# Two chained transformer blocks on one core: longer give-way times between the steps of the woven attention items

## Chip, cores and metric

The kernel runs as one program on one core of a Trainium2 chip. The metric is the device time of one execution in microseconds (us), where lower is better. The kernel before takes 3177.6 us, the median of three runs.

## What is computed

The reference runs two blocks in sequence on 512 tokens of width 1024, all in float32. The change touches only the attention part of the first block:

```
h = h + 0.5 * swiglu(rmsnorm(h))                       # feed-forward 1
u = rmsnorm(h)
(nq, kc, vc, ksl, vsl, kwn, vwn, ng, sq, sk, sv, ga, gb) = split(u @ w_in)
o_a = nsa(nq, ...)      # 8 heads, 2 key groups: compressed + selected + window attention, gated
o_b = banded(sq, sk, sv, window=128, sinks)            # 8 heads, 1 key head
merged = sigmoid(ga) * (o_a @ w_branch_a) + sigmoid(gb) * (o_b @ w_branch_b)
h = h + merged @ w_out
h = h + 0.5 * swiglu(rmsnorm(h))                       # feed-forward 2
...                                                    # then the second block
```

With 512 tokens, 8 selection blocks and 16 picks, the selected branch sees every earlier token, and so does the window branch with its window of 512. Both are plain causal attention here. The second block (a gated recurrence, a state-space model and a layer of 16384 small experts) follows and is not touched.

## The kernel before

Activations are kept transposed, 128 features by 512 tokens to a tile. Each weight tile of 128x1024 is loaded, split into a rounded part `whi` (ScalarE, line 171) and a rest `wlo` (VectorE, line 172), and multiplied in three passes by `mm3`: a product of a full weight tile, called a projection below, is 24 matmuls of 512 columns on TensorE.

The attention stage is written as Python generators that the planner `weave` interleaves while the program is built. There is one main stream and a list of 20 items. Main does the projections in a fixed order. Those before the items are the compression inputs, the keys, the queries and the four `natural`-layout tiles. Then come two compression products (`compress`, 48 matmuls of 256 columns each), five projections for the banded branch (`sk`, `s0` to `s3`), sixteen projections for the branch gates (lines 800 to 804), eight half-length products of the banded branch's output (`ob`), eight of the other branch (`oa`, lines 805 to 817), and the output projection. Each projection of main hands back after every six matmuls.

An item is the attention of one 128-token query tile for one branch: `full_item` (12 of them), `cmp_item` (compressed keys, 4) and `swa_item` (banded, 4). The order of query tiles is 3, 2, then the four banded items, then 1 and 0. At most two items are open at a time. An item emits all of its scores and its softmax (max and scaling on VectorE, exp on ScalarE), then yields. Then it goes into `attend`: it transposes the probabilities of the first block of 128 keys on TensorE (line 86) and copies them out of PSUM (`evac`, line 654, ScalarE and VectorE in turn), then yields. After that, for each block of keys it emits the next block's transposes and copies and this block's value product on TensorE, and yields.

A yield carries a number of nanoseconds on the planner's own clock `clk`. That clock does not run with time: it goes forward only when something is emitted on TensorE, by the cost that `mm` and `tr` put on it.

```
p = 4 if lhsT.dtype == F32 else 1
self.clk += max(n * 0.4217 * p, m * 0.84 * (2 if p == 4 else 1))    # mm: n columns, m columns of lhsT
...
self.clk += 54                                                      # tr
...
due[0] = v if callable(v) else self.clk + (v or 0)                  # weave, after an item yields v
```

So a yield of 5500 says: do not come back before 5500 ns' worth of other TensorE work was emitted, which is the other open item's or main's. `weave` always takes an item that is due before it takes main; if nothing but items is left it moves the clock on. By this clock one full projection costs 24 x 512 x 0.4217 ns = 5.18 us. The order of emission is the order of priority on each engine's queue.

Working tiles of 128x512 come from one set of 44 buffers (tag `t2k`), PSUM from 8 banks (tag `ps`). The gate projections leave one `t2k` tile each that lives until its branch product.

Of the kernel before, what the change touches and what calls it, by code (L numbers as in the profile page):

```python
# [49 lines left out]
class Prog:  # L50
# [165 lines left out]
    def small(self, n, w=4):  # L216
        t = self.big.tile([128, 64], F32, tag="rs_small", bufs=3, name=self.name("rs"))
        return [t[:, w * i:w * i + w] for i in range(n)]
# [439 lines left out]
    def attend(self, box, col, probs, width, v_of):  # L658
        if "po" not in box:
            box["po"] = self.ps()  # L660
        po = box["po"]
        nb = max(1, width // 128)
        nh = len(probs[0])
        n = min(128, width)
        cs = slice(col, col + 128 * nh)

        def turn(kb):
            r = []
            pts = [self.ps(), self.ps()]
            for pt, pr in zip(pts, probs):  # L670
                for i, p in enumerate(pr):
                    self.transposed(pt, i, p[:, kb * 128:kb * 128 + n], n)
            for pt in pts:
                s = self.t2k()
                self.evac(s[:n, :128 * nh], pt[:n, :128 * nh])
                r.append(s)
            return r

        t = turn(0)
        yield 1200  # L680
        for kb in range(nb):
            nxt = turn(kb + 1) if kb + 1 < nb else None
            start = not box["begun"]
            box["begun"] = True
            box["left"] -= 1
            for i in range(2):
                self.mm(po[64 * i:64 * i + 64, cs], lhsT=v_of(i, kb), rhs=t[i][:n, :128 * nh], start=start,
                        stop=box["left"] == 0)
            t = nxt
            if box["left"] == 0:  # L690
                box["done"]()
            yield 900

    def attention(self, st, done):
        nc, A, ph = self.nc, self.A, self.ph
# [151 lines left out]
        def cmp_item(box, qt):  # L847
            qs = slice(qt * 128, (qt + 1) * 128)
            m8 = small([128, 8, 31], "cm", 2)
            scs = [self.ps(), self.ps()]  # L850
            s4 = [sc[:, 0:128].rearrange("p (r n) -> p r n", r=4)[:, :, 0:31] for sc in scs]
            for r in range(4):
                for g, gp in enumerate(gps):
                    self.mm(s4[g][:, r, :], lhsT=nq[r][gp, qs], rhs=kcc[gp, g, :], start=True, stop=True)
            for g in range(2):
                nc.vector.tensor_tensor(m8[:, 4 * g:4 * g + 4], s4[g],
                                        self.misc["cmp"][:, qt, :][:, None, :].to_broadcast([128, 4, 31]), op=ALU.add)
            mx = small([128, 8], "mx", 6)
            sums = small([128, 8], "sums", 6)
            nc.vector.tensor_reduce(mx, m8, axis=AX.X, op=ALU.max)  # L860
            nc.vector.tensor_scalar(mx, mx, -0.125, None, op0=ALU.mult)
            for r in range(8):
                nc.scalar.activation(m8[:, r, :], m8[:, r, :], AF.Exp, bias=mx[:, r:r + 1], scale=0.125,
                                     accum_out=sums[:, r:r + 1])
            f = small([128, 8], "fac", 6)
            nc.vector.reciprocal(f, sums)
            nc.vector.tensor_tensor(f, f, gates[:, qt, 0:8], op=ALU.mult)
            if qt == 0:
                nc.vector.tensor_tensor(f, f, self.misc["vis"].to_broadcast([128, 8]), op=ALU.mult)
            nc.vector.tensor_tensor(m8, m8, f[:, :, None].to_broadcast([128, 8, 31]), op=ALU.mult)  # L870
            yield 4500
            yield from self.attend(box, 0, [[m8[:, 4 * g + r, :] for r in range(4)] for g in range(2)], 31,
                                   lambda g, kb: vcc[:, g, :])

        def full_item(box, qt, br, heads):
            qs = slice(qt * 128, (qt + 1) * 128)
            kT, off = ((ksl, 0), (kwn, 128))[br]
            nk = (qt + 1) * 128
            nh = len(heads)
            per = max(1, 512 // nk) if nk != 384 else 1  # L880
            mx = small([128, 8], "mx", 6)
            sums = small([128, 8], "sums", 6)
            probs = [[], []]
            for i in range(0, nh, per):
                scs = [self.ps(), self.ps()]
                for j in range(per):
                    for sc, gp in zip(scs, gps):
                        self.mm(sc[:, j * nk:(j + 1) * nk], lhsT=nq[heads[i + j]][gp, qs], rhs=kT[gp, :nk],
                                start=True, stop=True)
                for g, sc in enumerate(scs):  # L890
                    s3 = sc[:, :per * nk].rearrange("p (h n) -> p h n", h=per)
                    nc.vector.tensor_tensor(s3[:, :, qs], s3[:, :, qs],
                                            mdiag[:, None, :].to_broadcast([128, per, 128]), op=ALU.add)
                    k = g * nh + i
                    ms = mx[:, k:k + per]
                    nc.vector.tensor_reduce(ms, s3, axis=AX.X, op=ALU.max)  # L896
                    nc.vector.tensor_scalar(ms, ms, -0.125, None, op0=ALU.mult)
                    p = self.t2k()
                    for j in range(per):
                        pj = p[:, j * nk:(j + 1) * nk]  # L900
                        nc.scalar.activation(pj, s3[:, j, :], AF.Exp, bias=mx[:, k + j:k + j + 1], scale=0.125,
                                             accum_out=sums[:, k + j:k + j + 1])
                        probs[g].append(pj)
            f = small([128, 8], "fac", 6)
            nc.vector.reciprocal(f[:, :2 * nh], sums[:, :2 * nh])
            c = 8 * br + 8
            fv = f[:, :2 * nh].rearrange("p (g r) -> p g r", g=2)
            gv = gates[:, qt, c:c + 8].rearrange("p (g r) -> p g r", g=2)[:, :, heads[0]:heads[0] + nh]
            nc.vector.tensor_tensor(fv, fv, gv, op=ALU.mult)
            for g in range(2):  # L910
                for r in range(nh):
                    nc.vector.tensor_scalar(probs[g][r], probs[g][r], f[:, g * nh + r:g * nh + r + 1], None, op0=ALU.mult)
            yield 5500
            yield from self.attend(box, 128 * heads[0], probs, nk,
                                   lambda g, kb: nat[:, kb, off + g * 64:off + g * 64 + 64])

        def swa_item(box, qt):
# [34 lines left out]
            for par in range(2):  # L952
                for r in range(4):
                    nc.vector.tensor_scalar(probs[par][r], probs[par][r], f[:, 4 * par + r:4 * par + r + 1], None,
                                            op0=ALU.mult)
            yield 6000
            yield from self.attend(box, 0, probs, nw, lambda par, kb: nat[:, ks.start // 128 + kb, 256:320])

        items = []
# [3 lines left out]
        for qt in self.att_order:  # L963
            if qt >= 4:
                items.append((swa_item(accum(ob, "ob", qt - 4, 1 if qt == 4 else 2), qt - 4), need_s))
                continue
            hs = [range(4)] if qt < 2 else [range(0, 2), range(2, 4)]
            box = accum(oa, "oa", qt, 2 * (qt + 1) * len(hs) + 1)
            for br in range(2):
                for h in hs:  # L970
                    items.append((full_item(box, qt, br, list(h)), need))
            items.append((cmp_item(box, qt), need_c))
# [938 lines left out]
```

## Time and profile before

| | |
|---|---|
| median of three runs | 3177.6 us (3174.46 to 3178.54) |
| the profiled execution | 3182.49 us, of which the span of its instructions is 3180.5 us |
| TensorE (PE) | busy 3061.3 us, 96% of the span |
| VectorE (DVE) | busy 2044.6 us, 64% |
| ScalarE (ACT) | busy 1164.7 us, 37% |
| GpSimd (POOL) | busy 1084.8 us, 34% |
| mean granted TensorE clock | 0.98 of full |

The share of busy time is an average over stages. The attention stage runs from about 395 to 835 us of the span. A stop of TensorE is idle time ahead of one of its instructions; the profile names what ended it. The granted clock has two levels, 1.2 and 2.4 GHz, and a window's figure is the mean over its time.

### The profile page before, as it was taken

The page shows a single profiled execution, that of the slowest core. Times are in us where ns is not written, and L with a number is a line of the kernel's source. Part 1 is how long each engine was busy: PE and PEld are TensorE (multiplying, and loading weights), DVE is VectorE, ACT ScalarE, POOL GpSimd, SP SyncE. Part 2 cuts the span into 40 slices and gives each one's busy share as a digit, 9 for nine tenths or more (in the row PEclk, how much of TensorE's full clock was granted, in tenths as well). Part 3 has the DMA queues.
Part 4 walks back from the last instruction along what each step waited for, and adds up shares of the span by engine and source line. Part 5 has one row for each costly group of instructions (what it writes and reads, how often), then busy time and mean ns, then how long its engine had stood idle before and what let it go on. Part 6 is the DMA issues. An engine that isn't in the chain of part 4 may idle for free.

```text
span 3180.5 us, 39943 instructions
## 1 busy us (share of the span) xinstructions
PE 3061.3 (96%) x14672; PEld 2493.6 (78%) x14672; DVE 2044.6 (64%) x3733; ACT 1164.7 (37%) x1851; POOL 1084.8 (34%) x993
## 2 busy tenths in 40 slices
PE   8999998889999999999999988999999999999998
PEld 7888875567777778878888777888887788888887
DVE  7445466754657565864665899888883666555653
ACT  4222334442422224543433343445453333322332
POOL 1000110001222222431254689878771533223321
PEclk9999999999999999989999999999999999999999
DMA  6344331112435444221333344555556765555642
GB/s 197 118 131 136 94 96 47 34 47 86 160 101 170 131 141 133 85 77 54 100 121 116 103 150 168 189 188 188 191 186 225 244 200 184 185 194 193 201 135 78
DMA packets 145059, 443.53 MB, mean 139 GB/s; under 512 B 20177, under 2 KB 22257, under 8 KB 139745
## 3 DMA queue, kind: packets, MB, share of 16 engines
q1 hardware_dynamic: 82512, 285.41, 28.0%
q10 hardware_dynamic: 51968, 111.57, 9.7%
q0 software_dynamic: 10384, 44.01, 4.5%
q8 instruction: 116, 1.90, 0.2%
q14 instruction: 79, 0.64, 0.1%
HBM read 361.88 MB, written 77.86 MB: 138 GB/s over the span
## 4 chain that ended last, share of the span: by engine, by line
PE 78%; DVE 11%; issue 4%; ACT 2%; POOL 2%; DMA 2%; ACTq 0%; SPq 0%; DVEq 0%; POOLq 0%
PE ps L82 77%; DVE wlo L172 2%; DVE b L1543 1%; PE ps L86 1%; DMA aw<-ada_w 1%; ACT whi L171 1%; DVE stage L1568 1%; DMA act_d<-t 1%; DVE sel L1526 0%; DVE mx L896 0%; POOL t L814 0%; DVE aa L521 0%; ACTq L1156 0%; POOL a L1542 0%; DVE eq L1519 0%
## 5 line engine op out<-in xcount | busy, mean ns | idle before, releaser
L171 ACT CAST whi<-raw 128x1024 fp32r<-128x1024 f32 (+2 forms) x505 | 516.6, 1025 | 1210.2 <-PE ps L82 918.3
L82 PE MATMUL ps<-xhi,whi 128*128 128x512 f32 (+1 forms) x2232 | 879.0, 395 | 26.0 <-ACT whi L171 14.5
L82 PE MATMUL ps<-xhi,wlo 128*128 128x512 f32 (+1 forms) x2232 | 868.1, 390 | 8.2 <-DVE wlo L172 8.2
L82 PE MATMUL ps<-xlo,whi 128*128 128x512 f32 (+1 forms) x2232 | 869.4, 390 | 0.8 <-DVE xlo L380 0.7
L172 DVE TENSOR_TENSOR wlo<-raw,whi 128x1024 fp32r<-128x1024 f32 (+2 forms) x470 | 596.7, 1270 | 161.2 <-ACT whi L171 151.4
L82 PEld LDWEIGHTS ps<-xhi,whi 128*128 128x128 f32 x2232 | 425.4, 191 | 117.2 <-ACT whi L171 15.4
L82 PEld LDWEIGHTS ps<-xhi,wlo 128*128 128x128 f32 x2232 | 424.3, 190 | 99.3 <-DVE wlo L172 10.5
L82 PEld LDWEIGHTS ps<-xlo,whi 128*128 128x128 f32 x2232 | 425.2, 191 | 81.4 <-issue 2.1
L1542 POOL TENSOR_SCALAR a<-iota,routeT 128x128 fp32r<-128x128 f32 x512 | 439.6, 874 | 103.1 <-PE ps L82 97.2
L82 PE MATMUL ps<-pwl,whi 128*128 128x512 f32 (+1 forms) x1048 | 408.6, 390 | 2.8 <-DVE pwl L589 2.8
L82 PE MATMUL ps<-pwh,whi 128*128 128x512 f32 (+1 forms) x1048 | 406.8, 388 | 3.3 <-ACT pwh L588 3.2
L82 PE MATMUL ps<-pwh,wlo 128*128 128x512 f32 (+1 forms) x1048 | 403.1, 385 | 0.0
L1660 POOL TENSOR_TENSOR t<-t,gt 128x512 f32<-128x512 f32 x128 | 201.5, 1593 | 419.2 <-DMA t<-act_d 317.7
L1543 DVE SCALAR_TENSOR_TENSOR b<-iota,routeT,routeG 128x256 fp32r<-128x256 f32 x512 | 251.8, 541 | 46.0 <-PE ps L82 46.0
L82 PEld LDWEIGHTS ps<-pwh,whi 128*128 128x128 f32 x1048 | 197.4, 188 | 48.1 <-ACT pwh L588 4.6
L1794 DVE SCALAR_TENSOR_TENSOR h<-ps,mod,h 128x512 f32<-128x512 f32 (+1 forms) x131 | 96.3, 735 | 214.8 <-PE ps L82 214.8
L82 PEld LDWEIGHTS ps<-pwl,whi 128*128 128x128 f32 x1048 | 197.6, 189 | 42.3 <-DVE pwl L589 4.5
L82 PEld LDWEIGHTS ps<-pwh,wlo 128*128 128x128 f32 x1048 | 197.4, 188 | 42.5 <-DVE wlo L172 0.4
L1567 ACT COPY stage<-ps 128x256 f32<-128x256 f32 x256 | 138.1, 643 | 174.3 <-PE ps L82 138.1
L589 DVE TENSOR_TENSOR pwl<-t,pwh 128x512 fp32r<-128x512 f32 x128 | 144.8, 1160 | 40.0 <-ACT pwh L588 35.9
L266 POOL TENSOR_TENSOR acc<-acc,sq 128x512 f32<-128x512 f32 x18 | 32.3, 1796 | 391.2 <-ACT sq L262 390.8
L1568 DVE TENSOR_TENSOR stage<-stage,ps 128x256 f32<-128x256 f32 x256 | 147.3, 623 | 8.2 <-ACT stage L1567 8.1
(401 smaller groups left out, 3859.6 us busy)
## 6 DMA issues: line engine op xcount, KB each, us to landing
raw<-pu SPq DMA_DIRECT2D x128, 512.0 KB, 3.5
raw<-pv SPq DMA_DIRECT2D x128, 512.0 KB, 3.5
act_d<-t ACTq DMA_DIRECT2D x128, 256.0 KB, 2.4
gates_d<-stage ACTq DMA_DIRECT2D x32, 1024.0 KB, 4.6
gt<-gates_d POOLq DMA_DIRECT2D x16, 2048.0 KB, 14.6
t<-act_d ACTq DMA_DIRECT2D x128, 256.0 KB, 3.6
aw<-ada_w SPq DMA_DIRECT2D x48, 512.0 KB, 4.5
raw<-g SPq DMA_DIRECT2D x44, 512.0 KB, 3.6
```

The costliest lines, as they stand in the source:

```text
L82: self.nc.tensor.matmul(out, lhsT=lhsT, rhs=rhs, start=start, stop=stop)
L86: self.nc.tensor.transpose(out, x, ident)
L171: nc.scalar.copy(hi[:, :n], raw[:, :n])
L172: (nc.gpsimd if self.pool_lo else nc.vector).tensor_tensor(lo[:, :n], raw[:, :n], hi[:, :n].bitcast(F32), op=ALU.subtract)
L266: nc.gpsimd.tensor_tensor(st["acc"], st["acc"], sq, op=ALU.add)
L589: self.nc.vector.tensor_tensor(lo, x, hi.bitcast(F32), op=ALU.subtract)
L1542: g.tensor_scalar(a[:, i, :], iota, T2[0][:, c], None, op0=ALU.is_equal)
L1543: v.scalar_tensor_tensor(b[:, i], iota[:, None, :].to_broadcast([128, 2, 128]), T2[1][:, c], TG[:, t + i, :, None].to_broadcast([128, 2, 1 ...
L1567: nc.scalar.copy(sv, pv[:, :, 0])
L1568: v.tensor_tensor(sv, sv, pv[:, :, 1], op=ALU.add)
L1660: g.tensor_tensor(f(t), f(t), gts[e // 8][:, :, e % 8, :], op=ALU.mult)
L1794: nc.vector.scalar_tensor_tensor(x, ps, P.mod[:, 40 + d:41 + d], x, op0=ALU.mult, op1=ALU.add)
```

## The change

Five numbers that the items yield are raised: between softmax and transposes for each of the three kinds of item, between the first transposes and what follows them, and between blocks of keys. Nothing else is edited; the instructions are the same, and their order on the engines is what differs.

```
@@ attend
         t = turn(0)
-        yield 1200
+        yield 2200
         for kb in range(nb):
...
-            yield 900
+            yield 1800
@@ cmp_item
-            yield 4500
+            yield 7000
             yield from self.attend(box, 0, ...)
@@ full_item
-            yield 5500
+            yield 7000
             yield from self.attend(box, 128 * heads[0], probs, nk, ...)
@@ swa_item
-            yield 6000
+            yield 7500
             yield from self.attend(box, 0, probs, nw, ...)
```

## Rows read from the trace of the kernel before

**Rows 1.** Page, part 1: busy us, share of the span, instructions.
```profile
PE 3061.3 (96%) x14672; PEld 2493.6 (78%) x14672; DVE 2044.6 (64%) x3733; ACT 1164.7 (37%) x1851; POOL 1084.8 (34%) x993
```

**Rows 2.** Windows: stretch, its length, busy us by engine, granted clock, DMA.
```profile
454.80:688.00 233.20, 203.01 (x1070) 127.62 (x1069) 164.61 (x468) 112.79 (x356) 6.38 (x5) 0.93 0.15 45
688.00:768.00 80.00, 80.00 (x349) 65.60 (x350) 31.66 (x44) 23.69 (x36) 0.00 (x0) 1.00 0.25 79
410.00:454.80 44.80, 44.46 (x216) 37.22 (x216) 21.76 (x26) 10.52 (x17) 9.39 (x6) 1.00 0.26 83
```

**Rows 3.** TensorE groups by shape, 454.8 to 688 us.
```profile
L82 PE MATMUL ps<-xhi,whi 128*128 128x512 f32 x89 | 40.0, 450 | 1.8 <-ACT t L901 1.8
...
L82 PE MATMUL ps<-xhi,wlo 128*128 128x512 f32 x89 | 38.1, 428 | 0.0
L82 PE MATMUL ps<-xlo,whi 128*128 128x512 f32 x89 | 37.8, 425 | 0.0
...
L82 PE MATMUL ps<-whi,t 128*62 128x256 f32 x61 | 13.0, 293 | 0.0
L82 PE MATMUL ps<-wlo,t 128*62 128x256 f32 x30 | 8.6, 285 | 0.6 <-DVE wlo L172 0.6
```

**Rows 4.** TensorE groups by shape, 688 to 768 us.
```profile
L82 PE MATMUL ps<-xhi,wlo 128*128 128x512 f32 x80 | 31.2, 391 | 0.0
L82 PE MATMUL ps<-xlo,whi 128*128 128x512 f32 x79 | 30.7, 389 | 0.0
L82 PE MATMUL ps<-xhi,whi 128*128 128x512 f32 x79 | 30.7, 389 | 0.0
```

**Rows 5.** Waits of TensorE, 454.8 to 688 us: in total, times, longest.
```profile
PE ps L82 <- ACT t L654: 10.9, 6, 3.9
PE ps L86 <- DVE cm L870: 3.5, 1, 3.5
PE ps L86 <- DVE t L912: 2.7, 3, 1.5
PE ps L86 <- DVE t L954: 2.7, 1, 2.7
PE ps L86 <- ACT t L588: 2.6, 1, 2.6
PE ps L82 <- ACT t L901: 2.3, 3, 1.8
PE ps L82 <- ACT t L944: 2.1, 2, 1.4
PE ps L86 <- ACT t L901: 2.1, 2, 1.9
```

**Rows 6.** Timeline of VectorE and TensorE around the longest stop.
```profile
526.39 0.55 DVE L896 TENSOR_REDUCE mx<-ps 128x1 f32<-128x384 f32 x1
...
527.12 1.21 DVE L172 TENSOR_TENSOR wlo<-raw,whi 128x1024 fp32r<-128x1024 f32 x1
...
528.90 0.41 DVE L654 COPY t<-ps 128x256 f32<-128x256 f32 x1
...
530.00 1.12 PE L82 MATMUL ps<-t,nat 128*64 128x256 f32 x4 [3.90 <-ACT t L654]
```

**Rows 7.** Windows of 5 us around two stops.
```profile
525.00:530.00 5.00, 1.10 (x8) 0.62 (x6) 4.55 (x14) 3.27 (x9) 0.00 (x0) 0.90 0.16 17
530.00:535.00 5.00, 5.00 (x16) 2.81 (x17) 2.11 (x7) 0.60 (x2) 0.00 (x0) 0.50 0.24 91
535.00:540.00 5.00, 5.00 (x26) 2.96 (x25) 1.45 (x3) 0.75 (x2) 1.26 (x1) 0.92 0.00 0
...
655.00:660.00 5.00, 1.97 (x20) 0.97 (x16) 3.89 (x13) 3.28 (x21) 0.00 (x0) 1.00 0.00 0
660.00:665.00 5.00, 4.58 (x23) 3.08 (x24) 3.64 (x14) 3.52 (x17) 0.00 (x0) 1.00 0.00 0
```

**Rows 8.** VectorE and ScalarE groups by shape, 454.8 to 688 us.
```profile
L172 DVE TENSOR_TENSOR wlo<-raw,whi 128x1024 fp32r<-128x1024 f32 x20 | 25.4, 1272 | 2.1 <-ACT whi L171 1.9
...
L802 DVE TENSOR_TENSOR t<-ps,rb 128x512 f32<-128x512 f32 x5 | 3.3, 665 | 0.0
...
L171 ACT CAST whi<-raw 128x1024 fp32r<-128x1024 f32 x20 | 20.9, 1051 | 8.6 <-PE ps L82 7.8 <-ACT t L944 0.5 <-ACT whi L171 0.3
...
L803 ACT ACTIVATE t<-t 128x512 f32<-128x512 f32 x5 | 3.2, 636 | 2.8 <-DVE mx L861 2.0 <-DVE fac L909 0.5 <-DVE t L802 0.4
```

## The prediction, written before the change was run

> **What bounds the kernel now.** I read the page's busy shares first. The reader is to see that TensorE is busy for 96% of the span [rows 1], so that only time in which it stops, or runs at the lower clock, is to be had. Then I cut the attention stage into windows [rows 2]. Before the items (410 to 454.8 us) TensorE is busy 44.46 of 44.80 us, and after them (688 to 768 us) 80.00 of 80.00 us, both at clock 1.00. Between, while the 20 items are open, it is busy 203.0 of 233.2 us at a mean clock of 0.93. All loss that the change can touch lies there: 30.2 us idle, and, since 7% of the clock is missing, 0.07 x 233.2 = 16.3 us of work that would not be there at full clock. Together 46.5 us, 1.5% of the kernel. This is the most that can be gained.
>
> Third, the groups of TensorE instructions say who filled that window: 3 x 89 = 267 matmuls of main's projections, or 11.1 projections, and 61 + 30 = 91 of compression [rows 3]. In the window behind it 79 + 80 + 79 = 238 projection matmuls remain, 9.9 gate projections, with no stop at all [rows 4]. So main has work in hand when the items end, at a place where it covers nothing.
>
> Fourth, the waits name the stops [rows 5]: value products wait 10.9 us for the copies of line 654; transposes wait 3.5 + 2.7 + 2.7 + 2.6 + 2.1 = 13.6 us for probabilities in eight stops; scores and others wait 2.3 + 2.1 = 4.4 us for exps that release what they need. These are the three places at which an item yields too little, except the last, which has no yield.
>
> **What the change adds in cover.** On the planner's clock the yields of all items add up before to: halves of tile 3, 4 x (5.5 + 1.2 + 4 x 0.9) = 41.2; of tile 2, 4 x 9.4 = 37.6; tile 1, 2 x 8.5 = 17.0; tile 0, 2 x 7.6 = 15.2; compressed, 4 x 6.6 = 26.4; banded, 8.1 + 3 x 9.0 = 35.1; in all 172.5 us. The change adds 12 x 1.5 + 4 x 2.5 + 4 x 1.5 between softmax and transposes, 20 x 1.0 behind the first transposes and 45 x 0.9 behind blocks: 34 + 20 + 40.5 = 94.5 us.
>
> The items' own cost on that clock does not change. A half of tile 3, for one, has 4 scores of 512 columns at 0.864 us, 16 transposes at 0.054 and 8 value products of 256 at 0.432: 7.77 us. All items come to 31.1 + 23.3 + 15.5 + 7.8 + 27.2 + 15.5 = 120.4 us. Two items are open at a time, so the stretch grows by half of 94.5, 47.2 us, and as the items' work is fixed, main fills all of it: 47.2 / 5.18 = 9.1 projections.
>
> Does this clock describe the trace? Main's part of the window is 267 x 0.216 + 91 x 0.108 + 5 rotations at 0.864 = 71.7 us, with the items 192.1 us. Two slots of that are 384.2 us, of which 172.5 are yields and 120.4 own work. The remaining 91.3 us are 85 returns that came late, 1.1 us each, which is what main's grain of six matmuls (1.3 us) and the other item's bursts make. I keep them; 20 us more or less would be 10 us, two projections.
>
> Main's work is therefore moved, not added: 9.1 x 24 = 219 matmuls, at 80.00 us / 349 = 0.229 us each [rows 2] 50.1 us, leave the window behind and enter the items' window. The sum there is zero but for the stops and the clock. Of the 9.9 projections 0.8 remain behind the items, and then 96 matmuls of the `ob` product, 22 us, in front of the `oa` product that needs the last item. That tile's copies and splits are some eight operations of this size on either engine, 0.64 to 0.67 us each by the nearest rows [rows 8], so they stay hidden; with main used up they would cost about 5 us.
>
> **What the cover is worth, stop by stop.** If a moved matmul costs the waiting step nothing, each stop shrinks by its own yield's increase. The six stops on line 654 give at most 1.0 each, 6.0. The stop of 3.5 on the compressed item gives 2.5, the three of 2.7 in all (none over 1.5) all of it, the stops of 2.7 and 2.6 give 1.5 each, the two of 2.1 (longest 1.9) 1.7: 9.9. Together 15.9 us [rows 5].
>
> But main's projections are not free for the items. Each puts 1.27 + 0.67 = 1.94 us on VectorE and 1.05 + 0.64 = 1.69 us on ScalarE [rows 8] for 5.18 us of cover. The longest stop shows why that counts [rows 6]: the copies for which TensorE waits until 530.0 stand on VectorE at 528.90, behind the other item's max of 0.55 us and behind a `wlo` of 1.21 us. At 1.94 / 5.18 = 0.37, the relief is 0.63 of the cover: 3.8 on line 654 and 1.6 + 2.2 + 0.95 + 0.95 + 1.15 = 6.8 on the transposes, 10.6 us.
>
> The Trainium skill ("PSUM — Partial Sum Buffer", Engine vs sequencer instructions) says that ScalarE and VectorE take their queues strictly in order, which speaks against this change; by it alone the lower sum would hold, 10.6 us. The order in [rows 6] agrees with it.
>
> The 4.4 us of scores have no yield of their own. They may gain nothing, or up to 2 us, as the two open items are spread over a longer stretch. So idle time falls by 10.6 to 17.9 us; I take 14, between, because only part of the stops stand behind main's own work.
>
> The clock: around the longest stop three windows stand at 0.90, 0.50 (the level of 1.2 GHz throughout) and 0.92, (0.10 + 0.50 + 0.08) x 5 = 3.4 us lost beside the 3.9 us stop. Around 660 us, with a stop of 3.5, it stays at 1.00 [rows 7]. So not each stop costs clock, and a shorter one need not give it back. Bounds: nothing, and the share of the idle time saved, 17.9 / 30.2 x 16.3 = 9.7 us. I take the share for 14 us, 14 / 30.2 x 16.3 = 7.6 us: nearer to the upper end, since idle time and lost clock stand in the same windows.
>
> Sum: -14 - 7.6 = -22 us, with bounds of -10.6 and -27.6. The profiled execution took 3182.5 us (2.0 more than its span), 4.9 above the median, so the same subtraction is made from the median: 3177.6 - 22 = 3156 us, -0.7%, and 3150 to 3167 for this case.
>
> **Rivals.**
> 1. Nearly all stops go (gain of 28 to 46.5 us, about 3140). For it: two items that stand closer to each other than to main queue behind each other on VectorE, as in [rows 6], and more room between their steps can undo this beyond the yield itself. Against it: VectorE is busy 164.6 of 233.2 us, 0.71, and the moved work brings 9.1 x 1.94 = 17.7 us for a stretch of some 260 us: (164.6 + 17.7) / 260 = 0.70. It is no less crowded.
> 2. The moved casts eat the relief (between 10 us of gain and 6 us of loss, about 3174). The steps meet in other places than before; a different order makes other stops of the same kind. For it: the same share of VectorE as just worked out. Against it: eight of the stops are between softmax and transposes, where the yield grows by 1.5 to 2.5 us and most stops are no longer than that.
> 3. Slower: the 44 working tiles run out. At the items of query tile 1 there live 2 keys, 4 queries, 4 `oa` and 8 halves of `ob`, 18, and two items with 4 probability and 4 transposed tiles each, 16. Before, at most 5 gate tiles stand beside them, as line 802 ran 5 times in the whole window [rows 8]: 39. After, with 9 to 10 gates done by then, 43 to 44. One more, and an exp or a gate waits for a tile that the other item gives back. Such a stop would be like the longest one, 3.9 + 3.4 = 7.3 us [rows 5, 7]. Slower by 0.2% needs (22 + 6.4) / 7.3 = 4 of them; five give 3156 + 36 = 3192. Against it: the count only just reaches the number, and only for those items.
> That main runs dry I rule out: it needs 47.2 us and has 9.9 x 5.18 + 20.7 (the `ob` product) = 72 us on the planner's clock.
>
> **How the numbers follow.** Differences under 0.2%, 6.4 us, count as no change, which is about what a measurement of this kernel can tell. My forecast (gain of 10 to 28 us) has 0.52, rival 1 0.16, rival 2 0.21, rival 3 0.11. Faster: 0.52 + 0.16 + the part of rival 2 that lies above 6.4 us (3.6 of its 16 us), 0.05 = 0.73. No change: the rest of rival 2, 0.16. Slower: 0.11. The range of 3140 to 3181 leaves out the upper half of rival 1's gains (0.06), rival 3 (0.11) and a little of rival 2 (0.03), 2 in 10 in all.
>
> **What would show it.** In the trace after: the first scores still at about 455 us and the items' last value product at about 233 + 50 - 22 = 261 us later, near 716, instead of 688; some 480 projection matmuls between, instead of 267; line 802 about 14 times there; idle time of TensorE there about 16 us and a clock of 0.96 to 0.97; the dense stretch behind about 26 us long. Waits on line 654 fall to half, those on 912, 954 and 870 to a third. From the `oa` product on, nothing differs but the time at which it starts. The prediction is wrong if the items' window takes in main's matmuls but keeps 30 us of stops (rival 2), if stops appear whose releaser is the last user of a working tile (rival 3), or if the counts of main's matmuls in the window stay near 267 (the planner's clock then does not set the order).

## The result, and the profile after

The changed kernel takes 3145.55 us (median of four runs, 3144.09 to 3147.02). The kernel before took 3178.07 us beside it (four runs, 3174.46 to 3184.8). The ratio is 0.9895 with an interval of 0.9878 to 0.9913, a gain of 32.5 us, where 22 was forecast. The profiled executions, 3182.49 and 3144.09 us, stand 38.4 us apart, because that of before lies 4.4 us above its median. Sums over the trace are made against the 38.4.

The first line of the page after answers to [rows 1]. TensorE does the same 14672 instructions in a span that is 38.4 us shorter.

```profile
PE 3042.6 (97%) x14672; PEld 2481.3 (79%) x14672; DVE 2039.7 (65%) x3733; ACT 1161.8 (37%) x1849; POOL 1086.3 (35%) x993
```

The windows of after: the items, the dense stretch up to the first sum of the `oa` product (line 814), and the rest (columns as in [rows 2]).

```profile
454.80:701.40 246.60, 235.29 (x1288) 157.81 (x1288) 180.82 (x487) 123.90 (x372) 6.40 (x5) 1.00 0.18 57
701.40:731.80 30.40, 30.40 (x132) 24.57 (x131) 15.27 (x26) 9.46 (x17) 0.00 (x0) 1.00 0.28 87
731.80:3142.10 2410.30, 2333.18 (x11269) 1934.45 (x11268) 1598.80 (x2916) 881.18 (x1270) 1044.88 (x959) 0.98 0.46 153
```

The items start at the same 454.8 us and end at 701.4 instead of 688. TensorE is idle for 246.60 - 235.29 = 11.3 us there instead of 30.2, and the clock's mean is 1.00 instead of 0.93. The place where both kernels are again at the same work is line 814, in each kernel's trace:

```profile
L814 POOL TENSOR_TENSOR t<-t,t x8: 1602/1672/2201, 731.9 to 759.1; 128x512 f32<-128x512 f32 x8
```

```profile
L814 POOL TENSOR_TENSOR t<-t,t x8: 1575/1673/2198, 768.3 to 795.4; 128x512 f32<-128x512 f32 x8
```

The second is that of before. 768.3 - 731.9 = 36.4 us of the 38.4 are won by there. The rest of before, cut at the same work, is the window below, 2412.5 us against 2410.3. So all but 2 us lie in the stretch that the change touches.

```profile
768.00:3180.50 2412.50, 2335.14 (x11270) 1936.07 (x11268) 1603.38 (x2916) 881.34 (x1270) 1043.42 (x959) 0.98 0.46 153
```

The groups of TensorE by shape in the items' window of after answer to [rows 3]:

```profile
L82 PE MATMUL ps<-xhi,whi 128*128 128x512 f32 x162 | 69.2, 427 | 0.8 <-DVE t L654 0.8
L82 PE MATMUL ps<-xlo,whi 128*128 128x512 f32 x162 | 64.5, 398 | 0.0
L82 PE MATMUL ps<-xhi,wlo 128*128 128x512 f32 x162 | 64.3, 397 | 0.0
```

3 x 162 = 486 matmuls of main stand there, where 267 + 219 = 486 were forecast. Behind the items 3 x 6 = 18 are left (of [rows 4]'s 238), 0.75 of a projection, forecast 0.8. The groups of the window behind the items; in the last two stand the 96 matmuls of the `ob` product and the first 16 of `oa`:

```profile
L82 PE MATMUL ps<-xhi,whi 128*128 128x512 f32 x6 | 2.5, 408 | 0.0
L82 PE MATMUL ps<-xlo,whi 128*128 128x512 f32 x6 | 2.3, 391 | 0.0
L82 PE MATMUL ps<-xhi,wlo 128*128 128x512 f32 x6 | 2.3, 389 | 0.0
...
L82 PE MATMUL ps<-t,whi 128*128 128x512 f32 x75 | 23.7, 396 | 0.0
L82 PE MATMUL ps<-t,wlo 128*128 128x512 f32 x37 | 14.7, 396 | 0.0
```

So 18 + 96 = 114 matmuls that need none of the last items, some 26 us at 0.229 us each, were still in hand when the items ended.

The waits of TensorE in the items' window of after answer to [rows 5]:

```profile
PE ps L82 <- ACT t L654: 2.3, 5, 0.6
PE ps L86 <- DVE t L954: 2.1, 2, 1.7
PE ps L82 <- ACT t L901: 1.6, 2, 1.2
PE ps L86 <- DVE t L912: 1.5, 1, 1.5
PE ps L82 <- ACT whi L171: 1.3, 2, 0.7
PE ps L82 <- DVE t L654: 0.8, 1, 0.8
PE ps L86 <- ACT t L654: 0.7, 1, 0.7
```

Value products wait 2.3 us on line 654 instead of 10.9; transposes wait 2.1 + 1.5 us for probabilities, and 0.2 in a row not shown, instead of 13.6. No single stop is longer than 1.7 us, where before had one of 3.9 and one of 3.5. The windows of 5 us of after at the places of [rows 7]:

```profile
525.00:530.00 5.00, 4.08 (x16) 2.75 (x18) 4.32 (x16) 3.03 (x9) 0.00 (x0) 1.00 0.35 105
530.00:535.00 5.00, 5.00 (x26) 3.29 (x24) 3.46 (x9) 1.96 (x4) 0.00 (x0) 1.00 0.02 3
...
655.00:660.00 5.00, 3.52 (x18) 2.50 (x17) 3.96 (x15) 4.56 (x22) 0.00 (x0) 1.00 0.00 0
```

VectorE is about as busy as before, but the windows of TensorE at half clock are gone, here and in all others between 455 and 705 us.

### The profile page after: what moved, and what is told of

It is laid out like the page before. It is cut to its first block, busy times and chain, and to the rows that moved or that the text cites. A ratio compares the mean times of both kernels' runs of the same rounds, so it can differ in the third digit from the quotient of the medians.

```text
span 3142.1 us, 39934 instructions
## 1 busy us (share of the span) xinstructions
PE 3042.6 (97%) x14672; PEld 2481.3 (79%) x14672; DVE 2039.7 (65%) x3733; ACT 1161.8 (37%) x1849; POOL 1086.3 (35%) x993
## 4 chain that ended last, share of the span: by engine, by line
PE 63%; DVE 9%; issue 4%; POOL 2%; ACT 1%; DMA 1%; ACTq 0%; DVEq 0%; POOLq 0%
PE ps L82 63%; DVE b L1543 1%; DVE wlo L172 1%; PE ps L86 1%; DVE stage L1568 1%; DMA act_d<-t 1%; DVE sel L1526 1%; POOL t L814 0%; ACTq L1156 0%; DMA aw<-ada_w 0%; POOL a L1542 0%; ACT whi L171 0%; DVE eq L1519 0%; POOL t L996 0%; DVE aa L521 0%
## 5 line engine op out<-in xcount | busy, mean ns | idle before, releaser
L172 DVE TENSOR_TENSOR wlo<-raw,whi 128x1024 fp32r<-128x1024 f32 (+2 forms) x470 | 585.9, 1247 | 161.7 <-ACT whi L171 151.9
L589 DVE TENSOR_TENSOR pwl<-t,pwh 128x512 fp32r<-128x512 f32 x128 | 151.5, 1212 | 41.1 <-ACT pwh L588 37.0
```

The source lines that it names most:

```text
L172: (nc.gpsimd if self.pool_lo else nc.vector).tensor_tensor(lo[:, :n], raw[:, :n], hi[:, :n].bitcast(F32), op=ALU.subtract)
L589: self.nc.vector.tensor_tensor(lo, x, hi.bitcast(F32), op=ALU.subtract)
```

## The experiments

The numbers in one table first. "Idle" and "clock lost" are of the items' window of each kernel, which starts at 454.8 us in all: length minus TensorE's busy time, and (1 - clock) times length, so within 1.3 us or so, since the clock is given to two places. "Long stops" are those of 2 us or more, a line drawn here for counting only: how many the timeline of TensorE shows, and their sum. The last column is the median against that of before in the same comparison.

| kernel | window | idle | clock lost | long stops | time |
|---|---|---|---|---|---|
| before | 233.2 | 30.2 | 16.3 (0.93) | 6, 17.3 us | |
| the change | 246.6 | 11.3 | 0 (1.00) | 0 | -32.5 |
| e1 softmax yields only | 225.2 | 18.4 | 6.8 (0.97) | 3, 9.6 | -14.7 |
| e2 attend yields only | 241.6 | 22.8 | 9.7 (0.96) | 3, 11.2 | -15.0 |
| e3 half the step | 245.5 | 21.6 | 12.3 (0.95) | 3, 11.7 | -6.8 |
| e4 twice the step | 279.2 | 11.3 | 8.4 (0.97) | 1, 3.1 | -25.0 |
| e5 rests on GpSimd, before | 235.9 | 37.9 | 16.5 (0.93) | 7, 19.0 | +7.9 |
| e6 the same, after | 265.2 | 19.6 | 8.0 (0.97) | 3, 7.1 | -17.6 |
| e7 copies on ScalarE, before | 231.4 | 30.3 | 16.2 (0.93) | 6, 17.4 | +1.4 |
| e8 the same, after | 246.2 | 8.4 | 2.5 (0.99) | 0 | -35.4 |
| e9 no rest, before | 222.9 | 23.9 | 15.6 (0.93) | 3, 9.0 | -7.5 |
| e10 no rest, after | 242.4 | 7.5 | 0 (1.00) | 0 | -36.8 |
| e11 40 tiles, after | 246.6 | 11.5 | 2.5 (0.99) | 0 | -32.2 |
| e12 copies on ScalarE, other yields | 258.9 | 15.7 | 7.8 (0.97) | 2, 7.8 | -22.1 |

### e1 and e2: each half of the change alone

```
e1  attend:  yield 1200, yield 900   (as before)
    items:   yield 7000 / 7000 / 7500
e2  attend:  yield 2200, yield 1800
    items:   yield 4500 / 5500 / 6000   (as before)
```

> Only the three yields between softmax and transposes are raised (4500, 5500, 6000 to 7000, 7000, 7500); 1200 and 900 stay. A (each stop shrinks by its own step's yield): the 13.6 us of stops of transposes fall to about 4, the 10.9 us of value products behind the copies stay near 10; idle time of the items' window about 20 us, clock 0.96, gain 10 to 20 us. B (only the amount of main's work between counts, wherever it stands): 34 of 94.5 us added is 36% of the change, so stops of both kinds fall by about a third, gain 12 us. The kinds of stop tell them apart, not the time.

> Only the yields in attend are raised (1200 to 2200, 900 to 1800); those behind the softmax stay. A: the stops behind the copies of line 654 fall from 10.9 to 3 us or less, the transposes' 13.6 us stay at 10 or more; clock 0.95 to 0.97; gain 10 to 18 us. B: 64% of the added cover, stops of both kinds fall by two thirds, clock near 0.99, gain 21 us or more.

e1 took 3163.56 us (ratio 0.9948, interval 0.9921 to 0.9975), e2 3163.24 (0.9957, 0.9943 to 0.9972). Each is worth about half, and the two halves add up to the whole: 14.7 + 15.0 = 29.7 of 32.5, well within the intervals. The waits of TensorE in the items' window, first of e1, then of e2:

```profile
PE ps L82 <- ACT t L654: 11.2, 6, 3.7
PE ps L86 <- ACT t L944: 2.3, 1, 2.3
```

```profile
PE ps L82 <- ACT t L654: 7.6, 4, 4.6
PE ps L86 <- DVE cm L870: 4.5, 1, 4.5
PE ps L86 <- DVE t L954: 4.0, 3, 1.4
PE ps L86 <- DVE t L912: 2.6, 4, 1.5
```

The stops of the transposes belong to the yield behind the softmax. With it raised alone, the waits for 954, 912 and 870 fall from 8.9 us [rows 5] to 0.4, and of the waits for exps 2.3 us stay in one stop. Without it they are 11.1 us. The stops of the value products don't belong to the other yields in the same way: 7.6 us stay although each cover grew by 0.9 to 1.0, with a single stop of 4.6, longer than any of before. Together the two halves leave 2.3. The items' own part of the cover is not all that sets these stops.

Two windows of e2 around its stop of 4.5 us, which ends at 688.55, show what a stop costs in clock:

```profile
685.00:690.00 5.00, 1.45 (x7) 1.24 (x8) 2.08 (x5) 2.69 (x17) 0.00 (x0) 0.71 0.34 108
690.00:695.00 5.00, 5.00 (x17) 3.73 (x16) 1.28 (x2) 0.82 (x2) 0.00 (x0) 0.61 0.00 0
```

(0.29 + 0.39) x 5 = 3.4 us, as in the stretch of [rows 7] that loses 3.4 us beside its 3.9 us stop.

### e3 and e4: half the step and twice the step

```
e3  yields 1700, 1350 / 5750, 6250, 6750
e4  yields 3200, 2700 / 9500, 8500, 9000
```

> All five yields raised by half of the change. If stops shrink in proportion to the cover: idle time about 20 us, clock 0.96 to 0.97, gain 16 us. If the clock falls only behind long stops: most of the clock comes back at half the cover already, clock 0.98 to 0.99, gain 20 to 26 us.

> All five yields raised by twice the change (1200, 900, 4500, 5500, 6000 to 3200, 2700, 9500, 8500, 9000). By the planner's clock main has nothing left for the last two items, some 12 us of yields stand uncovered. A: stops among the earlier items fall to 5 us or less, the last two items cost about 10 us of idle time: the same as the change within 6 us, or slower than it by up to 10 us. If stops keep falling and the end costs nothing: another 8 us faster than the change.

e3 took 3171.46 us (0.9979, 0.9969 to 0.9989): 6.8 us for half the step, neither 16 nor 20 to 26. Its value products wait 12.6 us, more than before. ScalarE's timeline up to its stop of 4.46 us, and TensorE's row that ends it, show what it waits for:

```profile
593.12 0.48 ACT L944 ACTIVATE t<-ps,mx 128x256 f32<-128x256 f32 x1 [2.52 <-DVE mx L941]
...
594.93 1.05 ACT L171 CAST whi<-raw 128x1024 fp32r<-128x1024 f32 x1
...
598.27 0.20 ACT L948 ACTIVATE es<-es 128x8 f32<-128x8 f32 x1
598.37 0.58 ACT L654 COPY t<-ps 128x512 f32<-128x512 f32 x1
...
599.00 1.97 PE L82 MATMUL ps<-t,nat 128*64 128x512 f32 x4 [4.46 <-ACT t L654]
```

The copy for which TensorE waits stands behind the eight exps of a banded item, which began 5.2 us earlier, and one of main's casts. The long stops of line 654 that were read this way in the other kernels are built alike: e1 at 597.62 and 621.78, e2 at 617.70, e3 at 652.97, before at 596.68. Each time the other open item is in the middle of its softmax, and a row of its exps stands ahead of the copy on ScalarE (four in before's shorter stop, six to eight in the others). The Trainium skill ("PSUM — Partial Sum Buffer", Engine vs sequencer instructions) says that ScalarE and VectorE take their queues strictly in order; these timelines agree, the copy starts only behind the last of these exps.

This queue alone does not make the stop, though. The change has the same picture and hardly waits (the first and last rows are TensorE's, the others ScalarE's):

```profile
592.95 1.61 PE L86 MATMUL ps<-ident,t 128*128 128x128 f32 x8 [0.42 <-DVE t L954]
...
595.79 1.05 ACT L171 CAST whi<-raw 128x1024 fp32r<-128x1024 f32 x1 [4.20 <-issue]
596.75 0.47 ACT L944 ACTIVATE t<-ps,mx 128x256 f32<-128x256 f32 x1
...
601.24 0.58 ACT L654 COPY t<-ps 128x512 f32<-128x512 f32 x1
...
601.87 1.08 PE L82 MATMUL ps<-t,nat 128*64 128x512 f32 x4 [0.47 <-ACT t L654]
```

Eight exps and a cast stand ahead of this copy too, and eight exps again ahead of the copy at 613.90, whose product waits 0.64 us. The difference lies on TensorE. In the change its timeline has 30 of main's matmuls, about 7 us, between the transposes (until 594.6) and the product at 601.87. In e3 it has five, about 1 us, between the transposes (until 593.4) and the stop. So a long stop is what is left of the copy's delay when TensorE runs out of other work.

e4 took 3153.21 us (0.9925, 0.9905 to 0.9944), 7.7 us slower than the change, as the first expectation allows. Its windows up to and behind the last work that main can do beside the items, and two groups of its items' window:

```profile
454.80:718.40 263.60, 256.13 (x1358) 177.46 (x1354) 187.59 (x483) 124.74 (x363) 6.71 (x5) 0.99 0.19 61
718.40:740.00 21.60, 16.88 (x58) 9.29 (x58) 9.91 (x28) 7.28 (x26) 0.00 (x0) 0.60 0.08 25
```

```profile
L82 PE MATMUL ps<-t,whi 128*128 128x512 f32 x64 | 21.1, 410 | 0.0
L82 PE MATMUL ps<-t,wlo 128*128 128x512 f32 x32 | 12.6, 395 | 0.0
```

All 504 projection matmuls lie in e4's items' window (3 x 168 in its groups), and so do the 96 of the `ob` product. Main has nothing left, and from 718.4 us the last items wait bare: 4.7 us idle, and 0.40 x 21.6 = 8.6 us of clock lost. Up to there only 7.5 us were idle. The change, with 114 of these matmuls in hand at the end, stayed well clear of this, and no set between the two was run.

### e5 and e6: main's rests on GpSimd

The cast of `wlo` (line 172) goes to GpSimd for the projections beside the items, with the yields of before (e5) and after (e6).

```
+            self.pool_lo = True     # ahead of the natural-layout projections
...
+            self.pool_lo = False    # ahead of the branch products
```

> The yields of before, but from the natural-layout projections up to the branch products the weight rest wlo is made on GpSimd (2.4 us for 1024 columns, by the rows of the expert stage) and not on VectorE (1.27 us). T (main's casts on VectorE are part of what the items' steps wait for): 20 casts, 25 us, leave VectorE in the items' window; the stops behind copies and probabilities shrink by about a third, gain 6 to 12 us. R (the items' own softmax work of the other open item is what they wait for): stops and clock as before, within 5 us of before; a projection that waits for its rest costs up to 5 us.

> The changed yields with wlo on GpSimd in the same stretch. T: of the 11.3 us of stops that are left some 4 us go, 4 us faster than the change. R: within 3 us of the change.

e5 took 3185.76 us (1.0027, 1.0017 to 1.0036) and e6 3160.23 (0.9939, 0.9922 to 0.9955), which is about 15 us more than the change. Neither theory had this. The groups of VectorE by shape in e5's items' window (its line 914 is 912 of before, 898 is 896):

```profile
L914 DVE TENSOR_SCALAR t<-t,fac 128x512 f32<-128x512 f32 x16 | 17.2, 1135 | 0.0
L898 DVE TENSOR_REDUCE mx<-ps 128x1 f32<-128x512 f32 x16 | 10.8, 685 | 0.1
```

The same rows of before:

```profile
L896 DVE TENSOR_REDUCE mx<-ps 128x1 f32<-128x512 f32 x16 | 10.5, 681 | 0.1
L912 DVE TENSOR_SCALAR t<-t,fac 128x512 f32<-128x512 f32 x16 | 6.7, 478 | 0.0
```

The scaling of the probabilities takes 1135 ns instead of 478 while GpSimd casts; the max, which reads PSUM, stays. In e6 the scaling takes 879. The Trainium skill ("SBUF — State Buffer", Who interferes with whom) says that VectorE and GpSimd share one pair of ports as an exclusive lock, that a tensor_scalar can take it and that a tensor_reduce never contends on trn2. These rows agree. For the question asked, the price of main's casts, the experiment is spoilt: it put another delay in their place.

### e7 and e8: the copies on ScalarE alone

```
-                self.evac(s[:n, :128 * nh], pt[:n, :128 * nh])
+                self.nc.scalar.copy(s[:n, :128 * nh], pt[:n, :128 * nh])
```

> The yields of before; both copies of a block's transposes go to ScalarE instead of one to each engine. If the copies are late because VectorE is full (0.71 busy in the window, ScalarE 0.48): stops of value products fall from 10.9 to 5 us or less, gain 6 to 10 us. If they are late because either queue holds the other item's softmax in front of them, in order, and ScalarE's exps there wait for VectorE: stops stay at 8 to 13 us, time within 5 us of before or slower by the second copy's 0.4 to 0.6 us on ScalarE.

> The changed yields with both copies on ScalarE. By the first theory some 2 us faster than the change; by the second 2 to 6 us slower than it, as two copies in one queue take twice the time and the cover was made for one on each engine.

e7 took 3179.25 us (1.0004, 0.9994 to 1.0013), no difference. VectorE's busy time in the items' window falls from 164.6 to 142.8 us, its share from 0.71 to 142.8 / 231.4 = 0.62, and the wait for the copies hardly moves, 10.2 us in six stops instead of 10.9 in six. So a less full VectorE alone does not undo these stops, as the second expectation had it; the test is not a clean one, since the copies load ScalarE in exchange (0.48 to 0.55 of the window). e8 took 3142.44 us (0.9883, 0.9867 to 0.99), 3 us below the change, with intervals that overlap. That is nearer to the first expectation: the 2 to 6 us by which the second had it slower did not come.

### e9 and e10: no rest for main's projections beside the items

These tell what main's own casts cost the items. The kernels leave part of the computation out, as their expectations say.

```
+        if self.no_lo:
+            return raw, hi, hi
         lo = self.w.tile([128, 1024], F32R, tag="wlo", name=self.name("wlo"))
```

> The yields of before. From the natural-layout projections up to the branch products the weight rest wlo is left out: the third pass multiplies the rounded part once more, so the projections of that stretch are computed with a wrong rest, but all matmuls stand. 20 casts of 1.27 us leave VectorE in the items' window and no other engine gets them. T (main's casts on VectorE are part of what the items' steps wait for): stops fall from 30 to about 20 us and some clock comes back, gain 10 to 18 us. R (the other item's softmax is what they wait for): stops of 25 us and more, gain under 6 us.

> The changed yields, the rest left out in the same stretch. T: the 11.3 us of stops fall to 7 or less, 4 us or more faster than the change. R: within 2 us of the change.

e9 took 3169.19 us (0.9974, 0.9964 to 0.9984), 7.5 us less than before, between the two expectations. Its idle time falls by 6.3 us to 23.9, its clock stays at 0.93, and two of its waits are:

```profile
PE ps L83 <- ACT t L657: 8.7, 7, 2.8
PE ps L87 <- DVE mx L902: 3.6, 1, 3.6
```

(its line 657 is 654 of before.) e10 took 3139.88 us (0.9883, 0.9866 to 0.9899), 4.3 us below the change by the gains against before, with intervals that overlap; its 7.5 us of idle time are close to T. The casts are a part of the delay, as the prediction's tax of 0.37 has it, but the smaller part: without 20 of them on VectorE four fifths of the value products' wait remains.

### e11: fewer working tiles

```
-        P.n_t2k = 44
+        P.n_t2k = 40
```

> The change with 40 working tiles instead of 44. If the items with the longer yields hold close to 44 tiles (43 to 44 at query tile 1 by the count): some exps and gates wait for tiles, TensorE stops of 3 us and more come up in the second half of the window, 5 to 25 us slower than the change. If the count was too high: the same as the change within 3 us.

e11 took 3144.47 us (0.9896, 0.9879 to 0.9912), the same as the change, with the same waits to within 0.1 us. (It loses 1.7 us of clock behind a stop of 1.4 us, where the change has a stop of 1.5 us and loses none.) Four tiles fewer change nothing, so the 44 were not used up; rival 3's count was too high.

### e12: other yields

e8 with 0.2 to 0.4 us more in `attend` and 0.5 less behind the softmax.

```
yields 2600, 2000 / 6500, 6500, 7000; copies on ScalarE
```

> Both copies on ScalarE and the same total of cover as the change, but more of it in attend (2600 and 2000) and less behind the softmax (6500, 6500, 7000). If the value products' stops are the ones that need most cover: 1 to 4 us faster than the change with copies on ScalarE, about 3140. If the balance is right as it is: 2 to 8 us slower than that, as stops of transposes come back.

e12 took 3154.56 us (0.9928, 0.9912 to 0.9945), 13 us more than e8 by the gains against before. The value products, which have more cover than in e8, wait 8.2 us instead of 2.1, 5.2 of it in one stop. The timeline up to that stop (copies on its line 675):

```profile
604.52 0.47 ACT L944 ACTIVATE t<-ps,mx 128x256 f32<-128x256 f32 x1 [5.03 <-DVE mx L940]
...
606.33 1.05 ACT L171 CAST whi<-raw 128x1024 fp32r<-128x1024 f32 x1
...
609.07 0.25 ACT L948 ACTIVATE es<-es 128x8 f32<-128x8 f32 x1
609.17 1.11 ACT L675 COPY t<-ps 128x512 f32<-128x512 f32 x2
...
609.85 1.11 PE L82 MATMUL ps<-t,nat 128*64 128x512 f32 x1 [5.20 <-ACT t L675]
```

It is the picture of e3 again: eight exps of the other item and a cast, 4.7 us, ahead of the copies, and 18 of main's matmuls, 4.4 us, between the transposes and the stop. This contradicts the theory that each stop shrinks by its own yield's increase. Neither expectation had it: the transposes' stops did not come back (0.9 us behind line 912, 0.7 behind 901).

## Why the prediction was right, and where its sizes failed

The direction, the place and the moved work were right. The size was not: the gain of 32.5 us lies above the forecast case's 10 to 28 us and inside rival 1's 28 to 46.5, to which 0.16 had been given. That the stated range of 3140 to 3181 us holds the result is owed to the part of rival 1 in it.

**What bounds the kernel.** Right. 36.4 of 38.4 us came out of the 46.5 us that were found between 454.8 and 688 us, the rest stayed as it was.

**The moved work.** Right to the matmul: 486 in the items' window, 0.75 projection left, line 802 there 15 times (about 14 forecast). The planner's clock says how much of main goes beside the items. That it came out to the matmul is partly luck, as the prediction allowed for two projections more or less.

**The end of the items.** Forecast 233 + 50 - 22 = 261 us after their start, measured 246.6. With the same 50.2 us of moved work, 233.2 + 50.2 - 246.6 = 36.8 us were saved in the window: 18.9 idle (30.2 to 11.3) and 16.3 clock make 35.2 of it.

**Idle time.** 14 was the term, 18.9 the measurement. The transposes went as forecast: 6.8 to 9.9 of their 13.6 us were to go, 9.8 did, and e1 and e2 show that the softmax yield does it. The scores gave 2.8 of 4.4, a little more than the 2 us allowed. The value products were mis-sized: at most 6.0 us were to go, 8.6 did. The step that failed is "each stop shrinks by its own yield's increase". A long stop of theirs is a copy that stands behind the other item's softmax in an in-order queue for longer than TensorE has other work. The change's copies still stand there (601.24, 613.90), but 30 matmuls, 7 us, cover the first of them, where no yield of `attend` is over 2.2 us. e3, with yields of up to 1.7, has five matmuls there, and e12, with up to 2.6, has 18, and both stop for longer than before. So the work in between is not the size of the one yield.

The prediction had seen the queue in [rows 6], but read it on VectorE alone. The row of its stop names ScalarE's copy, and ScalarE's timeline of before has that copy behind an exp that waited for its max:

```profile
529.02 0.58 ACT L901 ACTIVATE t<-ps,mx 128x384 f32<-128x384 f32 x1 [1.05 <-DVE mx L897]
...
529.59 0.64 ACT L654 COPY t<-ps 128x256 f32<-128x256 f32 x2
```

It then priced the queue by main's casts (0.37 of the cover), which e9 shows to be the smaller part.

**The clock.** This is the larger miss: 7.6 us as a share of the idle time, bounded by 9.7, against 16.3, all of it. The step that failed is that the lost clock falls in proportion to the idle time: the 11.3 us of idle time that the change kept cost none. What the loss goes with instead is not settled. In the table it follows the long stops (16.3 us beside 17.3 us of them, 9.7 beside 11.2, 6.8 beside 9.6, and 0 to 2.5 in the four kernels without one) about as well as the idle time (30.2, 22.8, 18.4, and 7.5 to 11.5). Both relations are rough: e9 loses 15.6 us with 9.0 us of long stops, and e4 loses 8.4 with 11.3 us idle, most of it in the bare end. Windows of 5 us over the whole stretch tell more. Before loses clock in seven places, 1.7 us in each of four and 3.4 in each of three, each at or right behind a stop of 1.8 to 3.9 us; the change has no such place. But the length of a stop does not decide it: before has a stop of 3.5 us that cost nothing [rows 7], and e11 loses 1.7 us at one of 1.4. It was not taken apart by a run of its own.

**The rivals.** Rival 1's size is what came, a gain of 28 to 46.5 us. Its mechanism, room that undoes the queue beyond the yield itself, is half right: the effect goes beyond the yield, but the queue is not undone, it is covered (601.24). It was put at 0.16 because VectorE would be no less crowded. VectorE is indeed at 180.8 / 246.6 = 0.73, and the long stops went all the same, so this argument doesn't bear. Rival 2, other stops of the same kind, did not come with this set of yields but did with e3's and, in part, e12's. Rival 3 falls by e11. That main runs dry was rightly excluded, with 114 matmuls to spare; e4 shows the price.

**What stays open.** Why TensorE has 30 matmuls in hand there with these five numbers, and five or 18 with the neighbouring ones of e3 and e12, was not derived. It follows from the order that the planner writes out, and it was seen only as an outcome. Nor is it shown that another set would not do better.

## What to carry to other kernels

Raise give-way times while the filler work lasts, and not beyond it: the last items want something to hide behind (e4). Don't price such a change stop by stop. For each long stop compare two things in the timelines: what stands ahead of the waiting copy in the in-order queue of its engine, and how much other work TensorE has until then. Both follow from the whole order, so a stop can go or come as a whole with a small change of the numbers (6.8 us of gain instead of 32.5 with half the step). Measure several settings, and check in the timeline that the long stops are gone, and with them the places where TensorE loses clock.

## What the runs showed of the hardware that had not been expected

Beside casts on GpSimd, VectorE's scalings of 512 columns in SBUF went from 478 to 1135 ns on average (e5; the longest took 2.6 us, beside a cast of 2.6) and to 879 in e6. Those of 384 columns stayed at 478 in e5, where hardly any ran beside a cast, and took 683 in e6. The max from PSUM stayed (681, 685 and 686 ns). TensorE's granted clock stayed at 1.00 through 11.3 us of idle time in pieces of up to 1.7 us, and stood at 0.71 and 0.61 in the two windows around one stop of 4.5 us.
